# Plain fp32 products for the recurrent state of a state-space layer, and a second buffer for that state

## The chip, the core and the metric

The program runs on one core of a Trainium2 chip. A core has five engines that run side by side, each through its own list of instructions in a fixed order: TensorE (PE, matrix products, with PEld for the loading of its stationary operand), VectorE (DVE), ScalarE (ACT), GpSimd (POOL) and SyncE (SP, which here only issues transfers). An instruction waits until the semaphores that it names have been raised, and everything behind it on the same engine waits with it. The metric is the time of one execution on the device in microseconds (us), here the median of three runs. A profile is one execution taken by the hardware profiler.

## The reference, cut to what matters

Two layers are computed for 128 prompt tokens and 512 sample tokens. Layer 0 is attention, layer 1 a bidirectional state-space layer. The change touches only the chunked scan of layer 1:

```python
def ssd_chunked(x, a, b, c, h0):          # T tokens in chunks of 128, 4 groups of 8 heads
    a_cs = jnp.cumsum(a, axis=2)
    ...
    decay_end = jnp.exp(a_cs[:, :, -1:] - a_cs)
    states = jnp.einsum('bclgn,bclgrp->bcgrpn', b, x * decay_end[..., None])
    chunk_decay = jnp.exp(a_cs[:, :, -1])
    def step(h, inp):
        s, d = inp
        return h * d[..., None, None] + s, h
    h_final, h_prev = lax.scan(step, h0, (states, chunk_decay))
    y_off = jnp.einsum('bclgn,bcgrpn->bclgrp', c, h_prev) * jnp.exp(a_cs)[..., None]
    return y_diag + y_off, h_final
```

It is run forwards and backwards in time, with the same `b` and `c`. For each group of 8 heads the state `h` is a matrix of 128 (the state's width) by 512 (8 heads of 64). Each chunk reads it (`y_off`) and then replaces it by its decayed self plus that chunk's `states`.

## The kernel before

All large products have fp32 inputs that are split into a high and a low part (`split`, lines 72 to 74: the high part is a cast to the type fp32r on ACT, the low part is the input minus the high part, on DVE unless another engine is named). A product is then three products of parts, high by high, high by low and low by high, summed in PSUM. So it is for the projections (`proj_T`, line 914) and for the output product (`out_mm`, line 1400), and so it is, through `mm3` (lines 1010 to 1014), for the two products on the state. Products of smaller operands take fp32 as it is ("plain" below): the 128x128 product of B and C in `decay` (line 1131), the within-chunk product in `diag` (line 1149) and the prompt's final state (`prompt_state`, line 1175).

Layer 1 goes through 4 groups `g`. For a group, ten projections make x, B, C and z (`conv_chunk`, lines 994 to 999: three DVE steps, a tanh on ACT, one more DVE step). Then the scan runs over steps `j`, with `d` the direction:

- `weighted` (line 1163) makes x times its weights on POOL, and splits it into `xwh` and `xwl`;
- `off` (lines 1201 to 1208) multiplies C (`C0`, `C1` are its parts) by the state's parts `hh` and `hl`; DVE scales the result (line 1207), POOL adds it to `ys` (line 1208);
- `advance` (lines 1210 to 1217) multiplies B turned (`T0`, `T1`) by `xwh` and `xwl`; DVE multiplies the state by its decay in place (line 1215), adds the product (line 1216), and `h_split` splits the new state into `hh` and `hl` again.

`off` runs for four steps and two directions in each of 4 groups, 32 times; `advance` for three steps, 24 times. While the scan of group `g` runs, the projections of group `g + 1` are computed between its products (`fl`), so that TensorE has work while the scan waits. In the last group the output product takes their place.

The program is written in one order; a scheduler then sets the order of each engine's instructions by a cost model of its own, and puts in the waits. Tiles come from pools by tag: `hh`, `hl`, `xwh` and `xwl` have one buffer for each direction, `xw` one for both, and the state `h` one for each direction for the whole layer. PSUM tiles of the pool `pa` (tag `a`, 4 buffers) hold the products of the scan and all transposes; those of `pj` (2 buffers) the projections. At the layer's end the freed tiles hold parts of the output product's operand (`hold`) and of the gate (`mod_gate`).

In the trace a tile is named by its tag without what follows a figure: `h` is the state, and in rows of line 914 the projection's input.

Of the kernel before, what the change touches and what calls it, by code (L numbers as in the profile page):

```python
# [9 lines left out]
F32R = mybir.dt.float32r  # L10
AF = mybir.ActivationFunctionType
ALU = mybir.AluOpType
# [4 lines left out]
P = 128  # L17
D = 1024
KD = D // P
NT = 5  # L20
# [7 lines left out]
TW = 644  # L28
# [25 lines left out]
class Hybrid:  # L54
# [955 lines left out]
    def mm3(self, out, a, b, start=True, stop=True):  # L1010
        nc = self.nc
        nc.tensor.matmul(out, a[0], b[0], start=start, stop=False)
        nc.tensor.matmul(out, a[0], b[1], start=False, stop=False)
        nc.tensor.matmul(out, a[1], b[0], start=False, stop=stop)

    def layer1(self, hT, wp, pj, pa, ctx):
# [10 lines left out]
        bcs, xts, zss, W, Xw, H, Hs, St = {}, {}, {}, {}, {}, {}, {}, {}  # L1027
# [13 lines left out]
        def bc_unit(g, which):  # L1041
            if which == 0:
                wcur["bc"] = self.load_w(wp, A["l1_w_in"], [(2 * DI + P * g, P), (2 * DI + P * (NG + g), P)])
                bcs[g] = {"C": [self.tl(sp, [P, TW - 3], F32R, tag=f"C{i}") for i in range(2)]}
                bcs[g]["T"] = [self.tl(sp, [P, 4, P], F32R, tag=f"T{i}") for i in range(2)] + [self.tl(sp, [P, P], tag="T2")]
            u = wcur["u"] = bcs[g][which] = self.conv_chunk(16 + 4 * which + g, wcur["bc"], P * which, hT, pj, self.tl(sp, [P, TW - 3], tag=f"B{which}"))
            if which:
                self.split(*bcs[g]["C"], u, nc.gpsimd)

        def b_turn(g):  # L1050
            hi, lo, prompt = bcs[g]["T"]

            def put(t, ps):
                if t.start:
                    self.split(hi, lo, ps)
                else:
                    nc.scalar.copy(prompt, ps[:, 0, :])
            self.turn(bcs[g][0], pa, put)
# [97 lines left out]
        def weighted(g, t, d):  # L1156
            if t:
                xl = self.tl(wk, [P, 512], F32R, tag=f"xwl{d}", bufs=1)
                xh = self.tl(wk, [P, 512], F32R, tag=f"xwh{d}", bufs=1)
                xw = self.tl(wk, [P, 512], tag="xw", bufs=1)  # L1160
            else:
                xw = self.tl(wk, [P, 512], tag=f"xwl{d}", bufs=1)
            nc.gpsimd.tensor_tensor(h3(xw), h3(xts[g][:, t, :]), bch(self.ws[:, t, sl(g, d)]), op=ALU.mult)
            if t:
                self.split(xh, xl, xw)
                Xw[g, t, d] = (xh, xl)
            else:
                Xw[g, t, d] = xw

        def prompt_state(g, d):  # L1170
            xw = Xw.pop((g, 0, d))
            T = bcs[g]["T"]
            ps = self.tl(pa, [P, 4, P], tag="a")
            for j in range(4):
                nc.tensor.matmul(ps[:, j, :], xw[:, P * j:P * j + P], T[2], start=True, stop=True)
            st = self.tl(wk, [P, 4, P], tag="ym")
            nc.scalar.copy(st, ps)
            dst = O["new_state_f" if d == 0 else "new_state_b"][0, 8 * g:8 * g + 8].rearrange("h p n -> (h p) n").rearrange("(j q) n -> q j n", q=P)
            nc.sync.dma_start(out=dst, in_=st)
# [6 lines left out]
        def state_init(g, d):  # L1186
            st = St.pop((g, d))
            ps = self.tl(pa, [P, 4, P], tag="a")
            for j in range(4):
                nc.tensor.transpose(ps[:, j, :], st[:, j, :], self.ident)  # L1190
            h = H[d] = self.tl(sp, [P, 512], tag=f"h{d}")
            nc.scalar.copy(h, ps.rearrange("p j q -> p (j q)"))
            h_split(d)

        def h_split(d):
            hh = self.tl(wk, [P, 512], F32R, tag=f"hh{d}", bufs=1)
            hl = self.tl(wk, [P, 512], F32R, tag=f"hl{d}", bufs=1)
            self.split(hh, hl, H[d])
            Hs[d] = (hh, hl)

        def off(g, t, d):
            C = bcs[g]["C"]
            y = Y[:, t].rearrange("p j q -> p (j q)")
            ps = self.tl(pa, [P, 512], tag="a")
            self.mm3(ps, [C[i][:, ts(t)] for i in range(2)], Hs[d])
# [4 lines left out]
        def advance(g, t, d):  # L1210
            T = bcs[g]["T"]
            p2 = self.tl(pa, [P, 512], tag="a")
            self.mm3(p2, [T[i][:, t - 1, :] for i in range(2)], Xw.pop((g, t, d)))
            h = H[d]
            nc.vector.tensor_tensor(h3(h), h3(h), bch(self.cd[:, t, sl(g, d)]), op=ALU.mult)
            nc.vector.tensor_tensor(h, p2, h, op=ALU.add)
            h_split(d)
# [97 lines left out]
        def hold(t, q, tags, pool):  # L1315
            self.yT[t, q] = [self.tl(pool, [P, 4, P], F32R, tag=i, bufs=1) for i in tags]
            self.y_turn(t, q, wk, "u")
# [13 lines left out]
        for n in range(4, 6):  # L1331
            self.mod_gate(1, n, self.grow[1, n], pa, "a", wk, "xwh0", "xwl0")
# [10 lines left out]
        for k0 in range(0, 12, 2):  # L1343
# [3 lines left out]
            if k0 == 0:  # L1347
                hold(1, 1, ("hh0", "hl0"), wk)
                hold(4, 1, ("hh1", "hl1"), wk)
                hold(0, 1, ("xwh1", "xwl1"), wk)  # L1350
            elif k0 == 4:
                hold(1, 2, ("B0", "B1"), sp)
                hold(4, 2, ("C0", "C1"), sp)
                hold(0, 2, ("T0", "T1"), sp)
# [142 lines left out]
```

## Time and profile before

| | |
|---|---|
| Median of 3 runs | 1020.06 us (1019.86 to 1020.76) |
| Span of the profiled execution | 1016.4 us |
| Median less that span (start and end of a run, outside the trace) | 3.7 us |
| Busy share of the span: PE, PEld, DVE, ACT, POOL | 92%, 83%, 72%, 54%, 50% |
| Mean granted TensorE clock | 0.978 |

The profiled execution's own whole time is not listed, only its span from the first to the last instruction; 3.7 us is what lies around it if that execution was a median one. Busy time of PE counts a product from its start to its modelled end, which overlaps the start of the next one; the rate of a stream of products is therefore read from start to start. Layer 1's four groups lie at about 480 to 900 us, and the output product then takes the rest.

### The profile page before, as it was taken

The numbers are of one execution on the slowest core, as the hardware profiler recorded it, in microseconds if no ns is written. First come the engines' busy times: TensorE is split into PE (matmuls) and PEld (weight loads), VectorE is DVE, ScalarE is ACT, GpSimd is POOL, SyncE is SP. The second block draws the span as 40 slices with busy tenths as digits, with TensorE's granted clock in tenths as the row PEclk, the third lists the DMA queues.
The fourth block names the chain that finished last, engine by engine and source line by source line (L and its number), as shares of the span: only waits on it lengthen the run. The fifth ranks groups of instructions, "written<-read, shape, count | busy, mean of one in ns | idle before, by whom it ended". The sixth has DMA issues, their size and how long they took to land. (4 is left out here: it accounts for less than half of the span.)

```text
span 1016.4 us, 17297 instructions
## 1 busy us (share of the span) xinstructions
PE 939.4 (92%) x6522; PEld 847.7 (83%) x6522; DVE 727.0 (72%) x1094; ACT 549.4 (54%) x1272; POOL 503.2 (50%) x451
## 2 busy tenths in 40 slices
PE   5998999999999899989998898898988999889998
PEld 3898878989997789978997797788987999667786
DVE  5478665766776766757688788977688767996663
ACT  5346766757766653323465575567445664654340
POOL 3355325225450433445177679869487867642000
PEclk9999999999999999999999899998999999899999
DMA  9933242211122322333342345235324532446752
GB/s 312 350 120 104 92 142 89 84 52 43 42 64 84 104 87 102 125 100 96 99 137 91 104 147 171 68 129 160 111 90 133 178 110 89 135 147 193 256 194 100
DMA packets 90354, 127.91 MB, mean 126 GB/s; under 512 B 6816, under 2 KB 65312, under 8 KB 90272
## 3 DMA queue, kind: packets, MB, share of 16 engines
q1 hardware_dynamic: 90272, 126.82, 39.0%
q8 instruction: 51, 0.84, 0.3%
q14 instruction: 31, 0.25, 0.1%
HBM read 115.10 MB, written 11.70 MB: 125 GB/s over the span
## 5 line engine op out<-in xcount | busy, mean ns | idle before, releaser
L914 PE MATMUL pj<-h,wh 128*128 128x322 f32 (+1 forms) x1248 | 293.5, 320 | 6.2 <-DVE B L999 4.2
L74 POOL TENSOR_TENSOR wl<-raw,wh 128x512 fp32r<-128x512 f32 (+1 forms) x70 | 135.6, 1949 | 183.5 <-ACT wh L73 183.3
L914 PEld LDWEIGHTS pj<-h,wh 128*128 128x128 f32 (+1 forms) x1248 | 214.9, 192 | 11.0 <-issue 4.4
L914 PE MATMUL pj<-h,wl 128*128 128x322 f32 (+1 forms) x624 | 198.0, 318 | 0.0
L73 ACT CAST wh<-raw 128x1024 fp32r<-128x1024 f32 (+1 forms) x117 | 103.3, 912 | 81.8 <-DMA raw<-in_l_w_out 26.0
L914 PEld LDWEIGHTS pj<-h,wl 128*128 128x128 f32 (+1 forms) x624 | 120.2, 193 | 1.2 <-issue 0.2
L1140 ACT ACTIVATE am<-am,nb 128x128 f32<-128x128 f32 x320 | 98.6, 392 | 28.4 <-POOL am L1135 14.2
L283 PE MATMUL pp<-wh,big 128*128 128x256 f32 x576 | 113.4, 287 | 0.5 <-ACT sg L527 0.5
L283 PEld LDWEIGHTS pp<-wh,big 128*128 128x128 f32 x576 | 92.4, 191 | 0.7 <-ACT sg L527 0.7
L74 DVE TENSOR_TENSOR wl<-raw,wh 128x1024 fp32r<-128x1024 f32 x47 | 68.9, 1470 | 26.7 <-ACT wh L73 26.6
L283 PE MATMUL pp<-wl,big 128*128 128x256 f32 x288 | 81.8, 284 | 0.0
L74 DVE TENSOR_TENSOR pl<-pt,ph 128x512 fp32r<-128x512 f32 (+1 forms) x100 | 59.2, 600 | 25.9 <-ACT ph L73 25.0
L633 DVE TENSOR_REDUCE nm<-S 128x1 f32<-128x640 f32 x64 | 52.4, 820 | 13.6 <-PE S L630 12.7
L73 ACT CAST ph<-pt 128x512 fp32r<-128x512 f32 (+1 forms) x100 | 51.3, 518 | 18.8 <-PE pt L658 14.1
L637 ACT ACTIVATE Pt<-S,nm 128x640 f32<-128x640 f32 x64 | 51.3, 803 | 12.1 <-PE pt L658 9.5
L1141 POOL TENSOR_TENSOR am<-am,am 128x1024 f32<-128x1024 f32 x20 | 50.2, 2512 | 14.6 <-ACT am L1140 14.0
L1208 POOL TENSOR_TENSOR ys<-ys,ym 128x512 f32<-128x512 f32 x32 | 48.8, 1533 | 13.6 <-DVE ym L1207 13.6
L283 PEld LDWEIGHTS pp<-wl,big 128*128 128x128 f32 x288 | 55.0, 191 | 0.0
L658 PE MATMUL pt<-cst,Pt 128*128 128x128 f32 x320 | 50.8, 276 | 2.7 <-DVE pl L74 2.3
L630 PE MATMUL S<-kT,qT 128*128 128x320 f32 x256 | 50.6, 322 | 1.4 <-ACT Pt L637 1.4
L841 PE MATMUL a<-wh,big 128*128 128x256 f32 x256 | 46.8, 283 | 0.0
L658 PEld LDWEIGHTS pt<-cst,Pt 128*128 128x128 f32 x320 | 36.6, 141 | 11.9 <-PE S L630 3.8
(375 smaller groups left out, 2319.8 us busy)
## 6 DMA issues: line engine op xcount, KB each, us to landing
raw<-in_l_w_in SPq DMA_DIRECT2D x48, 512.0 KB
am<-acd SPq DMA_DIRECT2D x40, 512.0 KB
raw<-in_l_w_out SPq DMA_DIRECT2D x36, 512.0 KB
og<-in_l_mod_w SPq DMA_DIRECT2D x29, 512.0 KB
raw<-in_l_w_in SPq DMA_DIRECT2D x25, 256.0 KB
mw<-in_l_mod_w SPq DMA_DIRECT2D x11, 512.0 KB
raw<-in_l_mod_w SPq DMA_DIRECT2D x8, 512.0 KB
yzd<-ys SPq DMA_DIRECT2D x6, 640.0 KB
```

Of the source, the lines that this page charges most:

```text
L73: (heng.tensor_copy if heng else self.nc.scalar.copy)(hi, src)
L74: (eng or self.nc.vector).tensor_tensor(lo, src, r32(hi), op=ALU.subtract)
L283: nc.tensor.matmul(ps, a[:, k, cs], b[:, k, :], start=k == 0 and a is hi and b is w[0], stop=k == KD - 1 and a is lo)
L630: nc.tensor.matmul(S[:, 192 + 320 * q:512 + 320 * q], qTs[g, t][:, h, :], kT[:, hl, 320 * q:320 * q + 320], start=hl == 0, stop=hl == 1)
L633: nc.vector.tensor_reduce(c["m"], c["s"], axis=AX.X, op=ALU.max, negate=True)
L637: nc.scalar.activation(Pt, c["s"], AF.Exp, bias=c["m"], scale=1.0, accum_out=rss[g][t][:, h:h + 1])
L658: nc.tensor.transpose(pt[:, 2 * i + j, :], Pts[j][:, kt * P:kt * P + P], self.ident)
L841: self.nc.tensor.matmul(ps, self.ohl[a][:, k, ts], w[b][:, k, :], start=k == 0 and i == 0, stop=k == KD - 1 and i == 2)
L914: nc.tensor.matmul(ps[0:m, 190 + 322 * half:512 + 322 * half], w[b][:, k, off:off + m], hT[s][:, k, 322 * half:322 * half + 322], start=fi ...
L1140: nc.scalar.activation(af[d][:, h, :], af[d][:, h, :], AF.Exp, bias=self.nb[:, t, i:i + 1], scale=1.0)
L1141: nc.gpsimd.tensor_tensor(af[0], af[0], af[1], op=ALU.add)
L1208: nc.gpsimd.tensor_tensor(y, y, m, op=ALU.add)
```

## The change

The two products on the state become one plain fp32 product each. With `mm3` go all splits of the state, of the weighted x, of C, and of the turned B; the fp32 tiles of C (`bcs[g][1]`) and of the turned B (`T`, one tile for all five chunks now) are the operands. The state is no longer updated in place: each step takes a new buffer of two (`bufs=2`), the decay's product goes from the old into the new one, and the sum is made in the new one. The weighted x gets two buffers for each direction. The tags of `hold` and `mod_gate` follow. In the changed kernel's own numbering the product of `off` is line 1172 and its scaling 1174, the product of `advance` is line 1179, the decay 1182 and the sum 1183; `conv_chunk` keeps its lines.

```diff
-    def mm3(self, out, a, b, start=True, stop=True):
-        nc = self.nc
-        nc.tensor.matmul(out, a[0], b[0], start=start, stop=False)
-        nc.tensor.matmul(out, a[0], b[1], start=False, stop=False)
-        nc.tensor.matmul(out, a[1], b[0], start=False, stop=stop)
...
-            if which:
-                self.split(*bcs[g]["C"], u, nc.gpsimd)
...
-            hi, lo, prompt = bcs[g]["T"]
-
-            def put(t, ps):
-                if t.start:
-                    self.split(hi, lo, ps)
-                else:
-                    nc.scalar.copy(prompt, ps[:, 0, :])
-            self.turn(bcs[g][0], pa, put)
+            T = bcs[g]["T"]
+            self.turn(bcs[g][0], pa, lambda t, ps: nc.scalar.copy(T[:, t, :], ps))
...
+            xw = Xw[g, t, d] = self.tl(wk, [P, 512], tag=f"xw{d}", bufs=2)
             nc.gpsimd.tensor_tensor(h3(xw), h3(xts[g][:, t, :]), bch(self.ws[:, t, sl(g, d)]), op=ALU.mult)
-            if t:
-                self.split(xh, xl, xw)
-                Xw[g, t, d] = (xh, xl)
-            else:
-                Xw[g, t, d] = xw
...
-            h = H[d] = self.tl(sp, [P, 512], tag=f"h{d}")
-            nc.scalar.copy(h, ps.rearrange("p j q -> p (j q)"))
-            h_split(d)
-
-        def h_split(d):
-            hh = self.tl(wk, [P, 512], F32R, tag=f"hh{d}", bufs=1)
-            hl = self.tl(wk, [P, 512], F32R, tag=f"hl{d}", bufs=1)
-            self.split(hh, hl, H[d])
-            Hs[d] = (hh, hl)
+            H[d] = self.tl(wk, [P, 512], tag=f"h{d}", bufs=2)
+            nc.scalar.copy(H[d], ps.rearrange("p j q -> p (j q)"))
 
         def off(g, t, d):
-            C = bcs[g]["C"]
             y = Y[:, t].rearrange("p j q -> p (j q)")
             ps = self.tl(pa, [P, 512], tag="a")
-            self.mm3(ps, [C[i][:, ts(t)] for i in range(2)], Hs[d])
+            nc.tensor.matmul(ps, bcs[g][1][:, ts(t)], H[d], start=True, stop=True)
...
         def advance(g, t, d):
-            T = bcs[g]["T"]
             p2 = self.tl(pa, [P, 512], tag="a")
-            self.mm3(p2, [T[i][:, t - 1, :] for i in range(2)], Xw.pop((g, t, d)))
-            h = H[d]
-            nc.vector.tensor_tensor(h3(h), h3(h), bch(self.cd[:, t, sl(g, d)]), op=ALU.mult)
+            nc.tensor.matmul(p2, bcs[g]["T"][:, t, :], Xw.pop((g, t, d)), start=True, stop=True)
+            old, h = H[d], self.tl(wk, [P, 512], tag=f"h{d}", bufs=2)
+            H[d] = h
+            nc.vector.tensor_tensor(h3(h), h3(old), bch(self.cd[:, t, sl(g, d)]), op=ALU.mult)
             nc.vector.tensor_tensor(h, p2, h, op=ALU.add)
-            h_split(d)
```

The scheduler's order moves with it. On TensorE, at the second scan step of group 0, before: the parts of the state (`hh0`, `hl0` forwards, `hh1`, `hl1` backwards) by C, the weighted x by the turned B, and projections of group 1 (line 914).

```order
L1012 MATMUL a_1455_7037<-hh0_1434_6899,C0_1387_6598 128x512
L1013 MATMUL a_1455_7037<-hl0_1435_6900,C0_1387_6598 128x512
L1014 MATMUL a_1455_7037<-hh0_1434_6899,C1_1388_6599 128x512
L1012 MATMUL a_1457_7044<-hh1_1437_6909,C0_1387_6598 128x512
L1013 MATMUL a_1457_7044<-hl1_1438_6910,C0_1387_6598 128x512
L1014 MATMUL a_1457_7044<-hh1_1437_6909,C1_1388_6599 128x512
L1012 MATMUL a_1459_7051<-xwh0_1446_6962,T0_1389_6600 128x512
L1013 MATMUL a_1459_7051<-xwl0_1445_6961,T0_1389_6600 128x512
L1014 MATMUL a_1459_7051<-xwh0_1446_6962,T1_1390_6601 128x512
```

The same place on TensorE after the change, where B1 is C in fp32, T the turned B and xw0, xw1 the weighted x:

```order
L1172 MATMUL a_1437_6992<-h0_1422_6868,B1_1392_6663 128x512
L914 MATMUL pj_1456_7059<-h10_1183_5264,wh_1452_7049 128x322
L1172 MATMUL a_1439_6997<-h1_1424_6873,B1_1392_6663 128x512
L1179 MATMUL a_1441_7002<-xw0_1431_6924,T_1387_6598 128x512
L1179 MATMUL a_1443_7007<-xw1_1432_6926,T_1387_6598 128x512
```

Three instructions have become one in each product, and no instruction that waits for a low part stands between a state's product and the next. On DVE, at the same step before, from the last operation of a projection's chunk to the scaling of the decay matrix `am0`:

```order
L999 SCALAR_TENSOR_TENSOR u_1451_6973<-pj_1452_6974,u_1451_6973 128x641
L74 TENSOR_TENSOR hl0_1435_6900<-h0_1405_6747,hh0_1434_6899 128x512
L74 TENSOR_TENSOR hl1_1438_6910<-h1_1409_6758,hh1_1437_6909 128x512
L1215 TENSOR_TENSOR h0_1405_6747<-h0_1405_6747,cd_1346_6373 128x512
L74 TENSOR_TENSOR xwl1_1448_6967<-xw_1450_6969,xwh1_1449_6968 128x512
L1154 TENSOR_TENSOR ys_1310_6019<-ys_1310_6019,a_1442_6950 128x512
L1215 TENSOR_TENSOR h1_1409_6758<-h1_1409_6758,cd_1346_6373 128x512
L1142 TENSOR_TENSOR am0_1414_6797<-am0_1414_6797,cb_1440_6915 128x1024
```

And after the change on DVE, from the same operation of that chunk to the next chunk's first:

```order
L999 SCALAR_TENSOR_TENSOR u_1433_6928<-pj_1434_6929,u_1433_6928 128x641
L1174 TENSOR_TENSOR ym_1438_6994<-a_1437_6992,ea_1345_6372 128x512
L1174 TENSOR_TENSOR ym_1440_6999<-a_1439_6997,ea_1345_6372 128x512
L1183 TENSOR_TENSOR h0_1442_7004<-a_1441_7002,h0_1442_7004 128x512
L1182 TENSOR_TENSOR h0_1464_7134<-h0_1442_7004,cd_1346_6373 128x512
L1183 TENSOR_TENSOR h1_1444_7009<-a_1443_7007,h1_1444_7009 128x512
L1182 TENSOR_TENSOR h1_1466_7139<-h1_1444_7009,cd_1346_6373 128x512
L994 TENSOR_SCALAR u_1455_7058<-pj_1456_7059,cw_99_556,cols_21_110 128x641
```

The three low parts are gone from the step, and the decay of the next state (into its other buffer, `h0_1464` from `h0_1442`) follows the sum at once.

## Rows read from the trace of the kernel before

**Rows 1.** Page, busy time of an engine, its share of the span, instructions.
```profile
PE 939.4 (92%) x6522; PEld 847.7 (83%) x6522; DVE 727.0 (72%) x1094; ACT 549.4 (54%) x1272; POOL 503.2 (50%) x451
```

**Rows 2.** Busy time by stretch of layer 1: us, each engine, granted clock, DMA.
```profile
core 0: us, PE busy (x) PEld busy (x) DVE busy (x) ACT busy (x) POOL busy (x), PEclk, DMA share, GB/s
480.00:900.00 420.00, 387.62 (x2562) 358.08 (x2561) 336.71 (x366) 239.48 (x565) 300.29 (x193) 0.97 0.39 122
540.00:560.00 20.00, 15.83 (x81) 13.27 (x79) 19.46 (x20) 7.56 (x24) 14.40 (x10) 0.91 0.24 84
...
620.00:640.00 20.00, 16.09 (x102) 13.31 (x101) 19.02 (x18) 8.51 (x19) 20.00 (x14) 1.00 0.42 138
640.00:660.00 20.00, 16.22 (x86) 14.19 (x86) 20.00 (x21) 10.01 (x27) 15.59 (x10) 0.91 0.29 80
...
860.00:880.00 20.00, 15.19 (x89) 12.23 (x90) 20.00 (x22) 10.86 (x24) 15.24 (x10) 0.91 0.27 89
```

**Rows 3.** Waits of PE, 480 to 900 us: us in total, times, longest.
```profile
PE a L1013 <- DVE hl L74: 8.2, 7, 2.9
PE a L1012 <- DVE ys L1154: 4.7, 2, 2.7
PE pj L914 <- DVE B L999: 4.2, 3, 2.8
...
PE a L1013 <- DVE xwl L74: 2.4, 1, 2.4
PE a L1012 <- ACT hh L73: 2.3, 2, 1.3
...
PE a L1012 <- DVE h L1216: 0.8, 1, 0.8
```

**Rows 4.** Timeline of DVE from 538 us: start, us, operation, idle before.
```profile
539.30 4.66 DVE L74 TENSOR_TENSOR hl<-h,hh 128x512 fp32r<-128x512 f32 x2
543.89 2.87 DVE L1215 TENSOR_TENSOR h<-h,cd 128x512 f32<-128x512 f32 x1
```

**Rows 5.** Groups on DVE, 480 to 930 us: count, busy us, mean ns, idle before.
```profile
L74 DVE TENSOR_TENSOR hl<-h,hh 128x512 fp32r<-128x512 f32 x32 | 41.6, 1315 | 3.6 <-ACT hh L73 3.3
...
L1215 DVE TENSOR_TENSOR h<-h,cd 128x512 f32<-128x512 f32 x24 | 28.0, 1174 | 0.0
L74 DVE TENSOR_TENSOR xwl<-xw,xwh 128x512 fp32r<-128x512 f32 x24 | 27.9, 1161 | 3.3 <-ACT xwh L73 3.3
...
L1216 DVE TENSOR_TENSOR h<-a,h 128x512 f32<-128x512 f32 x24 | 16.3, 677 | 0.0
```

**Rows 6.** Timeline of PE: one product in three parts, and the next start.
```profile
530.04 0.40 PE L1012 MATMUL a<-xwh,T 128*128 128x512 f32 x1
530.28 0.39 PE L1013 MATMUL a<-xwl,T 128*128 128x512 f32 x1
530.51 0.40 PE L1014 MATMUL a<-xwh,T 128*128 128x512 f32 x1
530.75 0.39 PE L1012 MATMUL a<-xwh,T 128*128 128x512 f32 x1
```

**Rows 7.** Timeline of PE: plain products (two records each), and the next start.
```profile
486.55 0.43 PE L962 MATMUL a<-am,xs 128*128 128x160 f32 x2
486.82 0.43 PE L963 MATMUL a<-am,xs 128*128 128x160 f32 x2
...
585.14 1.05 PE L1175 MATMUL a<-T,xwl 128*128 128x128 f32 x8
586.03 0.39 PE L1131 MATMUL a<-B,B 128*128 128x128 f32 x2
```

**Rows 8.** Waits of DVE and of POOL, 480 to 930 us: us in total, times, longest.
```profile
DVE am L1142 <- POOL am L1141: 9.8, 6, 5.2
...
POOL xw L1163 <- DVE xwl L74: 11.4, 8, 2.6
```

More of the change, by code (lines that the diff above doesn't have):

```diff
@@ L1026, in layer1 @@
         Y = self.Y = self.tl(sp, [P, NT, 4, P], tag="ys")
-        bcs, xts, zss, W, Xw, H, Hs, St = {}, {}, {}, {}, {}, {}, {}, {}
+        bcs, xts, zss, W, Xw, H, St = {}, {}, {}, {}, {}, {}, {}
         wcur = {}
@@ L1043, in bc_unit @@
                 wcur["bc"] = self.load_w(wp, A["l1_w_in"], [(2 * DI + P * g, P), (2 * DI + P * (NG + g), P)])
-                bcs[g] = {"C": [self.tl(sp, [P, TW - 3], F32R, tag=f"C{i}") for i in range(2)]}
-                bcs[g]["T"] = [self.tl(sp, [P, 4, P], F32R, tag=f"T{i}") for i in range(2)] + [self.tl(sp, [P, P], tag="T2")]
-            u = wcur["u"] = bcs[g][which] = self.conv_chunk(16 + 4 * which + g, wcur["bc"], P * which, hT, pj, self.tl(sp, [P, TW - 3], tag=f"B{which}"))
-            if which:
-                self.split(*bcs[g]["C"], u, nc.gpsimd)
-        def b_turn(g):
-            hi, lo, prompt = bcs[g]["T"]
-            def put(t, ps):
-                if t.start:
-                    self.split(hi, lo, ps)
-                else:
-                    nc.scalar.copy(prompt, ps[:, 0, :])
-            self.turn(bcs[g][0], pa, put)
+                bcs[g] = {"T": self.tl(sp, [P, NT, P], tag="T")}
+            wcur["u"] = bcs[g][which] = self.conv_chunk(16 + 4 * which + g, wcur["bc"], P * which, hT, pj, self.tl(sp, [P, TW - 3], tag=f"B{which}"))
+        def b_turn(g):
+            T = bcs[g]["T"]
+            self.turn(bcs[g][0], pa, lambda t, ps: nc.scalar.copy(T[:, t, :], ps))
         def z_tile(g, jj):
@@ L1156, in weighted @@
         def weighted(g, t, d):
-            if t:
-                xl = self.tl(wk, [P, 512], F32R, tag=f"xwl{d}", bufs=1)
-                xh = self.tl(wk, [P, 512], F32R, tag=f"xwh{d}", bufs=1)
-                xw = self.tl(wk, [P, 512], tag="xw", bufs=1)
-            else:
-                xw = self.tl(wk, [P, 512], tag=f"xwl{d}", bufs=1)
-            nc.gpsimd.tensor_tensor(h3(xw), h3(xts[g][:, t, :]), bch(self.ws[:, t, sl(g, d)]), op=ALU.mult)
-            if t:
-                self.split(xh, xl, xw)
-                Xw[g, t, d] = (xh, xl)
-            else:
-                Xw[g, t, d] = xw
+            xw = Xw[g, t, d] = self.tl(wk, [P, 512], tag=f"xw{d}", bufs=2)
+            nc.gpsimd.tensor_tensor(h3(xw), h3(xts[g][:, t, :]), bch(self.ws[:, t, sl(g, d)]), op=ALU.mult)
         def prompt_state(g, d):
@@ L1174, in prompt_state @@
             for j in range(4):
-                nc.tensor.matmul(ps[:, j, :], xw[:, P * j:P * j + P], T[2], start=True, stop=True)
+                nc.tensor.matmul(ps[:, j, :], xw[:, P * j:P * j + P], T[:, 0, :], start=True, stop=True)
             st = self.tl(wk, [P, 4, P], tag="ym")
@@ L1315, in hold @@
         def hold(t, q, tags, pool):
-            self.yT[t, q] = [self.tl(pool, [P, 4, P], F32R, tag=i, bufs=1) for i in tags]
+            self.yT[t, q] = [self.tl(pool, [P, 4, P], F32R, tag=i, bufs=1 if tags[0] != tags[1] else 2) for i in tags]
             self.y_turn(t, q, wk, "u")
@@ L1331, in layer1 @@
         for n in range(4, 6):
-            self.mod_gate(1, n, self.grow[1, n], pa, "a", wk, "xwh0", "xwl0")
+            self.mod_gate(1, n, self.grow[1, n], pa, "a", wk, "xw0", "xw0", 2)
         part_mm(12)
@@ L1347, in layer1 @@
             if k0 == 0:
-                hold(1, 1, ("hh0", "hl0"), wk)
-                hold(4, 1, ("hh1", "hl1"), wk)
-                hold(0, 1, ("xwh1", "xwl1"), wk)
+                hold(1, 1, ("h0", "h0"), wk)
+                hold(4, 1, ("h1", "h1"), wk)
+                hold(0, 1, ("xw1", "xw1"), wk)
             elif k0 == 4:
@@ L1353, in layer1 @@
                 hold(4, 2, ("C0", "C1"), sp)
-                hold(0, 2, ("T0", "T1"), sp)
+                hold(0, 2, ("T", "T1"), sp)
             elif k0 == 8:
```

## Prediction

> **What bounds the kernel now.** I read the page's first part: TensorE (PE) is busy for 92% of the span and DVE for 72% [rows 1]. Such a share is a mean over stages, so I went on to the stretches of layer 1 [rows 2]. From 480 to 900 us, where the four scans lie, PE is busy for 387.6 of 420 us, and its idle 32.4 us are not spread evenly: from 540 to 560, 640 to 660 and 860 to 880 us PE falls to 15.8, 16.2 and 15.2 of 20 while DVE stands at 19.5, 20.0 and 20.0. There DVE is the bound. In the same three stretches the granted clock is 0.91: after each gap PE runs for a while at 1.2 instead of 2.4 GHz. Over the 420 us the clock is 0.97, and the 3% that lack are worth 0.03 x 420 = 12.6 us of full speed. So 32.4 + 12.6 = 45 us of PE's time is the most that can come back here.
>
> Next the waits name who held PE up [rows 3]. Waits on the parts of the operands that the change removes: 8.2 us for `hl`, 2.4 for `xwl`, 2.3 for `hh`, and 0.8 for the state itself, together 13.7. Waits on DVE work that has nothing to do with the split but stood in the same queue: 4.7 us for the sum into `ys` (line 1154, it frees a PSUM tile) and 4.2 for a chunk's last step (line 999), together 8.9. The timeline shows how the queue comes about [rows 4]: from 539.30 us two `hl` subtractions take 4.66 us, and the decay in place behind them 2.87 us. By the groups [rows 5] the sum with one operand in PSUM (line 1216) has a mean of 677 ns, while `hl`, `xwl` and the decay of the same size, whose operands all lie in SBUF, have 1315, 1161 and 1174 ns. They are lengthened by something, and they run while POOL is busy too [rows 2].
>
> **The change part by part.** *PE.* The split product on 512 columns costs 530.75 - 530.04 = 0.71 us from start to start in an unbroken stream [rows 6]. Plain products of 512 columns are not in this trace; narrower ones are [rows 7]: 160 columns go from 486.55 to 486.82, 0.27 us, which makes 0.86 us for 512, and four products of 128 columns take 586.03 - 585.14 = 0.89 us for 512 in all. From below, a plain product leaves two records, and if each passed at the split part's rate (0.71 / 3 = 0.24 us) it would cost 0.47 us. I take 0.87, between the two that were seen. There are 32 + 24 = 56 products, so PE gains work: 56 x (0.87 - 0.71) = +9.0 us (ends: -13.4 and +10.1). That is the surprise in this change: one instruction instead of three, and slower.
>
> The Trainium skill ("FP8 and Floating Point Precision", section TensorE Precision Notes) states that true fp32 makes four passes through the array. Four passes at 0.24 us are 0.95 us by an estimate from that page and the stream above, +13.3 us in all, and the sum below would end at 1009.2 us. The 0.27 us for 160 columns agree with four passes of 160 columns at 2.4 GHz, without the overhead of a split part's start.
>
> *DVE.* The 32 subtractions for `hl` and 24 for `xwl` go: 41.6 + 27.9 = 69.5 us of 336.7 in the stretch [rows 2, 5], 21% of DVE's load, and they lie just in the steps in which it is full. Without them the three full stretches would not be full. The state's path gets shorter by a cast and a subtraction: product, sum, next product.
>
> Of the 13.7 us of waits on parts I let 3 us return as waits on the sum alone: -10.7 us. Of the 8.9 us in DVE's queue I let three quarters go, because DVE's load falls by a fifth where it was at 97 to 100%: -6.7 us. With 17.4 of 32.4 us of idle time gone I take the same share of what the clock costs: 17.4 / 32.4 x 12.6 = -6.8 us. The other 10 us of idle time (waits on POOL's and ACT's results) I leave as they are.
>
> The Trainium skill ("SBUF — State Buffer", section Who interferes with whom) says that a DVE instruction with two SBUF inputs contends with a GpSimd instruction that reads SBUF, and that the loser is blocked until the other is through. That fits 1315 against 677 ns. By it the lengthening is a wait that the next such instruction inherits, so DVE would be relieved only by 56 x 0.677 = 38 us instead of 69.5; scaling the 6.7 us by that gives 3.7, the clock's share falls to 5.6, and the sum would end at 1009.
>
> *What I cost at nothing.* 60 casts on ACT (`hh`, `xwh`, the high part of C) and four subtractions on POOL go; ACT is busy for 239 of 420 us, so its work is hidden beside PE's, and this matters only through the waits counted above. The turned B is copied instead of cast, on the same engine. The second buffer of the state removes no wait of before: the decay in place never left DVE idle (0.0 in its group, [rows 5]). It prevents a new one: `off` now reads the state itself on PE, and a decay in place would have to wait for that product, with DVE's chunk steps queued behind it. With two buffers the decay waits for a product that was issued a step earlier. The two buffers of the weighted x free POOL from its 11.4 us of waiting for `xwl` [rows 8]; POOL's results then come a little earlier, which I don't count. The one wait on PE that takes the place of the old ones is that of `off` for the sum. Behind it stand the projections of the next group, whose results DVE, ACT and then the next weights' PSUM tiles wait for. In the new order of group 0 some 22 projection products (0.15 us each, by 322 of 512 columns of 0.24) stand between one step's products and the next `off`, over 3 us, against two sums and the decay between them, 0.68 us each, that DVE has to do meanwhile (the two scalings run beside the products of `advance`); DVE meets that when nothing else stands before them, so the 3 us that I let return are not zero. The end (`hold`, `mod_gate`) gets its tiles from tags whose last readers are scan products done before; if a reader were late, only the output product's operand would wait, a few us at most.
>
> *The sum.* +9.0 - 10.7 - 6.7 - 6.8 = -15.2 us. From the span 1016.4 - 15.2 = 1001.2, with 3.7 us around it 1004.9 us. The profiled execution is taken as a median one, since its span and those 3.7 us are set to make 1020.06.
>
> **The rivals.** *POOL sets the step.* With DVE freed, the scan waits for POOL, which multiplies x by its weights, masks and adds the decays and adds into `ys`. For it: POOL is busy for 20.0 of 20 us from 620 to 640 [rows 2], and DVE itself waited 9.8 us for its decay sums [rows 8]. Against it: over the stretch POOL has 300 of 420 us, and where PE was lowest (860 to 880) it has 15. Then the queue's waits stay and only those on parts go, with their share of the clock: -10.7 - 10.7 / 32.4 x 12.6 + 9.0 = -5.9, 1014.2 us.
>
> *PE pays and gets nothing back: slower.* TensorE is the bound at 92%, and each plain product holds it 0.16 us longer. If the new order lets `off` wait for the sum for as long as it waited for the parts (in the new order the four products of a step stand together, and the sum of the second direction comes last in DVE's queue), the whole +9.0 us stays: 1029.1 us. It decides for slower from the point at which less than 7 of the 45 us come back. Against it: 13.7 us are put down by name to what is removed.
>
> *Nothing to be seen.* 7 to 11 us come back and pay for the passes: 1018 to 1022 us.
>
> *All comes back.* PE is never idle and always at full clock: 9.0 - 45 = -36, 984 us. The same time comes out of the forecast if a plain product costs its lower end (-24.2 - 13.4 = -37.6, 982.5 us). Against the first: 10 us of idle time have other causes; against the second: both rows of plain products.
>
> **How the numbers follow.** Forecast (995 to 1012) 0.52; POOL's step (1012 to 1018) 0.16; all back or a cheap product (below 995) 0.11; nothing to be seen 0.08; slower 0.13. What a measurement of this kernel can tell from no change is about 0.2%, 2 us. So faster 0.52 + 0.16 + 0.11 = 0.79, same 0.08, slower 0.13. The range from 990 to 1022 leaves out the lower part of "all back" and most of "slower", some 0.18.
>
> **What would show it.** Right: in the new trace a plain product of 512 columns takes 0.85 to 0.9 us from start to start; DVE's busy time from 480 to 900 us falls by 40 to 70 us; no stretch of 20 us has DVE above 19; PE's idle time there is 15 us or less and the clock 0.98 or more; waits of PE on the sum of the state add up to about 3 us. Wrong: PE's idle time is as large as before and put down to the state's sum or to POOL; or the plain product costs 0.5 or 1 us, which moves the time by 56 times the difference.

## The result, and the profile after

The changed kernel takes 1005.42 us (median of 4 runs, 1004.66 to 1006.87) against 1019.96 us for the kernel before, run on the same chip (4 runs, 1015.28 to 1020.76). The ratio is 0.9874 with a 95% interval of 0.9852 to 0.9897: faster by 14.5 us, where 1004.9 us had been forecast. A later repeat of both gave 0.9883 (0.9851 to 0.9916). The span of the profiled execution fell from 1016.4 to 1003.1 us.

The page's line of busy times, after:

```profile
PE 935.6 (93%) x6466; PEld 832.5 (83%) x6466; DVE 667.6 (67%) x1034; ACT 515.1 (51%) x1212; POOL 500.0 (50%) x447
```

Against [rows 1], DVE lost 60 instructions and 59 us (the 56 subtractions and, not counted in the prediction, four for the low part of the turned B, 2.7 us together); PE has 56 records fewer (two for a product instead of three) and nearly the same busy time. The price of a plain product stands in the timeline of PE, after (start, duration, records):

```profile
523.05 1.88 PE L1172 MATMUL a<-h,B 128*128 128x512 f32 x4
524.77 1.02 PE L1179 MATMUL a<-xw,T 128*128 128x512 f32 x2
```

Four records are two products, and the next starts 1.72 us later: 0.86 us each, against 0.71 for three parts [rows 6].

The same stretches as in [rows 2], after:

```profile
480.00:900.00 420.00, 394.26 (x2562) 351.41 (x2561) 293.45 (x325) 213.14 (x518) 299.73 (x196) 0.98 0.41 127
540.00:560.00 20.00, 18.15 (x84) 14.03 (x83) 18.99 (x20) 8.50 (x25) 17.77 (x12) 0.91 0.35 105
620.00:640.00 20.00, 15.96 (x95) 13.26 (x95) 17.89 (x23) 9.03 (x22) 18.76 (x15) 0.91 0.39 117
860.00:880.00 20.00, 17.54 (x86) 13.33 (x86) 19.93 (x21) 10.65 (x22) 10.56 (x6) 0.91 0.52 171
```

DVE falls by 43 us, but one stretch is still full (19.93), and PE is still idle for 25.7 us. A fixed stretch compares unlike work, though: after, some 13 us of the output product's work have moved into it. The next two fences hold the same work, from the turning of B in group 0 to the last product of the output's first part; of before, and of after:

```profile
512.80:942.70 429.90, 393.62 (x2531) 356.55 (x2529) 351.27 (x385) 247.17 (x571) 299.85 (x204) 0.97 0.40 128
```

```profile
514.20:929.00 414.80, 389.84 (x2475) 342.00 (x2474) 292.74 (x325) 213.25 (x511) 296.18 (x200) 0.98 0.42 132
```

The instruction counts fit the change (2531 - 2475 = 56; 385 - 325 = 60). The work takes 15.1 us less: PE's idle time fell from 36.3 to 25.0 us, 11.3, and its busy time by 3.8, although the plain products add 56 x 0.15 = 8.4. DVE fell by 58.5 us.

Waits of PE from 480 to 900 us, after (us, times, longest):

```profile
PE a L1371 <- POOL ssq L1098: 4.3, 1, 4.3
PE a L1116 <- DVE h L1183: 4.0, 1, 4.0
PE pj L914 <- DVE B L999: 3.8, 3, 2.4
PE a L1137 <- DVE h L1183: 2.4, 1, 2.4
PE pj L914 <- DVE u L999: 1.8, 1, 1.8
```

Of [rows 3] the waits on parts are gone, and so is that on `ys`; the one on L999 is not. Two new ones name the sum L1183, 6.4 us together, but the waiting instructions are not products with the state: L1116 (B by C) and L1137 (the turning of `ys`) write into PSUM tiles of the same four buffers, and read nothing that the sum makes: what they lack is the tile that it empties.

Groups on DVE, 480 to 930 us, as in [rows 5], after; behind them three of before that were not shown:

```profile
L1127 DVE TENSOR_TENSOR am<-am,cb 128x1024 f32<-128x1024 f32 x20 | 40.0, 2001 | 6.7 <-POOL am L1126 6.2
L1182 DVE TENSOR_TENSOR h<-h,cd 128x512 f32<-128x512 f32 x24 | 28.8, 1211 | 0.1
L1086 DVE TENSOR_TENSOR ys<-ys,zs 128x512 f32<-128x512 f32 x12 | 18.3, 1534 | 0.3
L1183 DVE TENSOR_TENSOR h<-a,h 128x512 f32<-128x512 f32 x24 | 15.8, 679 | 1.5 <-PE a L1179 1.5
L1086 DVE TENSOR_TENSOR ys<-ys,zs 128x128 f32<-128x128 f32 x12 | 12.9, 1082 | 0.0
```

```profile
L1142 DVE TENSOR_TENSOR am<-am,cb 128x1024 f32<-128x1024 f32 x20 | 34.8, 1740 | 10.1 <-POOL am L1141 9.8
L1101 DVE TENSOR_TENSOR ys<-ys,zs 128x512 f32<-128x512 f32 x12 | 13.6, 1149 | 0.2
L1101 DVE TENSOR_TENSOR ys<-ys,zs 128x128 f32<-128x128 f32 x12 | 10.0, 842 | 0.1
```

Of the other operations with two SBUF inputs these got longer: the mask's product by 5.2 us in all, the gate by 4.7 and 2.9, the decay by 0.8, together 13.6. But one got shorter, the low part of the weights; over the same work, before and after:

```profile
L74 DVE TENSOR_TENSOR wl<-raw,wh 128x1024 fp32r<-128x1024 f32 x28 | 45.9, 1638 | 15.4 <-ACT wh L73 15.4
```

```profile
L74 DVE TENSOR_TENSOR wl<-raw,wh 128x1024 fp32r<-128x1024 f32 x28 | 38.7, 1382 | 12.0 <-ACT wh L73 12.0
```

With it and the smaller ones, the operations that are left took some 7 us more on balance. That is half of what lacks between the 72.2 us taken away (69.5 and 2.7) and the 58.5 that DVE was relieved of. For the other half an estimate is the overlap of neighbours, which busy time counts once: operations of 0.68 us start 0.60 us apart where they follow each other (619.48 to 620.08 in a timeline below), and 60 of them are gone. The sum with an operand in PSUM stayed at 679 ns.

What lengthens an operation can be read from these traces. In those of before, of the changed kernel and of the run with the subtractions put back (below), from 480 to 930 us, DVE has 184 operations of 128x512 with two SBUF inputs (low parts, decays, subtractions put back). Of the 55 beside which POOL was idle throughout, all took 0.67 to 0.69 us; all 104 that took over 0.75 us ran beside a busy POOL. Of the 168 with an input in PSUM (scalings and sums), all took 0.67 to 0.69 us, though POOL was busy for over half of the time of 124. So it is the two SBUF inputs beside a busy POOL.

### The profile page after: what moved, and what is told of

The parts are those of the page before. It is cut to its first block, busy times and chain, and to the rows that moved or that the text cites. A ratio compares the mean times of both kernels' runs of the same rounds, so it can differ in the third digit from the quotient of the medians.

```text
span 1003.1 us, 17041 instructions
## 1 busy us (share of the span) xinstructions
PE 935.6 (93%) x6466; PEld 832.5 (83%) x6466; DVE 667.6 (67%) x1034; ACT 515.1 (51%) x1212; POOL 500.0 (50%) x447
## 4 chain that ended last, share of the span: by engine, by line
PE 54%; DVE 14%; POOL 11%; issue 8%; DMA 7%; ACT 6%; SPq 0%; POOLq 0%; DVEq 0%; ACTq 0%
PE pj L914 14%; PE pp L283 8%; PE po L668 3%; PE a L841 3%; PE pj L1366 3%; PE acc L379 3%; PE S L630 3%; PE pt L658 3%; DMA am<-acd 2%; PE pp L175 2%; POOL ys L1175 2%; POOL am L1126 2%; POOL xw L1143 2%; DVE ys L1086 2%; ACT am L1125 2%
## 5 line engine op out<-in xcount | busy, mean ns | idle before, releaser
L914 PE MATMUL pj<-h,wh 128*128 128x322 f32 (+1 forms) x1248 | 299.4, 326 | 7.3 <-DVE B L999 3.8
L914 PEld LDWEIGHTS pj<-h,wh 128*128 128x128 f32 (+1 forms) x1248 | 212.3, 190 | 19.4 <-issue 12.6
L74 POOL TENSOR_TENSOR wl<-raw,wh 128x512 fp32r<-128x512 f32 (+1 forms) x70 | 131.8, 1893 | 185.1 <-ACT wh L73 183.4
L74 DVE TENSOR_TENSOR wl<-raw,wh 128x1024 fp32r<-128x1024 f32 x47 | 61.6, 1317 | 23.7 <-ACT wh L73 23.6
L1366 PE MATMUL pj<-wh,h 128*128 128x512 f32 x160 | 52.5, 402 | 1.0 <-ACT h L73 1.0
```

What stands on the lines that cost most here:

```text
L74: (eng or self.nc.vector).tensor_tensor(lo, src, r32(hi), op=ALU.subtract)
L914: nc.tensor.matmul(ps[0:m, 190 + 322 * half:512 + 322 * half], w[b][:, k, off:off + m], hT[s][:, k, 322 * half:322 * half + 322], start=fi ...
L1366: nc.tensor.matmul(self.PS[t][n], y[a][:, kk, :], b, start=k0 + k == 0 and i == 0, stop=k0 + k == 15 and i == 2)
```

## The experiments

Each ran beside the kernel before on its chip; since chips differ a little, the ratios to it are what is compared, and the kernel before has medians from 1015.98 to 1019.96 us on them.

**What a plain product costs TensorE.** First each plain product was issued twice, onto the same result:

```
-            nc.tensor.matmul(ps, bcs[g][1][:, ts(t)], H[d], start=True, stop=True)
+            for _ in range(2):
+                nc.tensor.matmul(ps, bcs[g][1][:, ts(t)], H[d], start=True, stop=True)
...
-            nc.tensor.matmul(p2, bcs[g]["T"][:, t, :], Xw.pop((g, t, d)), start=True, stop=True)
+            xw = Xw.pop((g, t, d))
+            for _ in range(2):
+                nc.tensor.matmul(p2, bcs[g]["T"][:, t, :], xw, start=True, stop=True)
```

> The changed kernel with each of the 56 plain products on the state issued twice into the same place of PSUM: 56 x 0.86 = 48 us more of TensorE's work, nothing more elsewhere. Theory (TensorE is the bound for most of the scan once VectorE is relieved): 30 to 48 us slower than the changed kernel, 1035 to 1053 us. Rival (another engine sets the scan's pace and TensorE's idle 26 us there take the work up): at most 25 us slower, 1030 us or less.

Measured: 1035.48 us, ratio 1.0176 (1.0143 to 1.0209), 30 us over the changed kernel. The timeline of PE in this kernel:

```profile
521.19 3.60 PE L1173 MATMUL a<-h,B 128*128 128x512 f32 x8
524.63 1.88 PE L1182 MATMUL a<-xw,T 128*128 128x512 f32 x4
```

Eight records, four products, 3.44 us: 0.86 again. The 56 more products are 48 us of PE's work, and 30 of them show. Over the same work PE's idle time is 13.0 us in this kernel, against 25.0:

```profile
512.40:958.60 446.20, 433.25 (x2586) 361.95 (x2585) 286.84 (x327) 214.21 (x511) 291.31 (x200) 0.99 0.39 123
```

So 12 of the other 18 us went into idle time; a part of the rest is the clock, 0.99 for 0.98.

Then the opposite, one pass in place of a plain product:

```
-                bcs[g] = {"T": self.tl(sp, [P, NT, P], tag="T")}
+                bcs[g] = {"T": self.tl(sp, [P, NT, P], F32R, tag="T")}
...
-            xw = Xw[g, t, d] = self.tl(wk, [P, 512], tag=f"xw{d}", bufs=2)
+            xw = Xw[g, t, d] = self.tl(wk, [P, 512], F32R, tag=f"xw{d}", bufs=2)
...
-            old, h = H[d], self.tl(wk, [P, 512], tag=f"h{d}", bufs=2)
+            old, h = H[d], self.tl(wk, [P, 512], F32R, tag=f"h{d}", bufs=2)
```

> The changed kernel with the four operands of the products on the state rounded to fp32r where they are made, and one product in one part: it leaves out the low parts, and with them part of the precision. TensorE loses 56 x (0.86 - 0.24) = 35 us of work, nothing else changes. Theory (the passes are paid in full): 20 to 35 us faster than the changed kernel, 970 to 985 us. Rival (VectorE and POOL set the pace in the scan, the passes are hidden beside them): 10 us or less, 995 us and up.

Measured: 976.57 us, ratio 0.961 (0.9577 to 0.9643). The timeline of PE:

```profile
521.33 0.63 PE L1172 MATMUL a<-h,B 128*128 128x512 f32 x2
521.79 0.39 PE L1179 MATMUL a<-xw,T 128*128 128x512 f32 x1
```

Two products in 0.46 us, 0.23 each: 56 x (0.86 - 0.23) = 35 us less work, and 29 us less time (27 by the ratios). Work on TensorE shows for the greater part, 29 of 35 here and 30 of 48 there, and the step of the sum that charged the passes holds. The forecast had worked with four passes of 0.24 us as one of its cases (the Trainium skill, "FP8 and Floating Point Precision", section TensorE Precision Notes). By an estimate from that page, reckoned as the forecast did on 160 columns, four passes of 512 columns at 2.4 GHz take 4 x 512 / 2.4 = 853 ns, and the measured 0.86 us agrees. Too dear in that case of the forecast were the 0.24 us for a pass.

**Is it VectorE's load that came back as time?** The 56 subtractions were put back on DVE, with two SBUF inputs and results that nothing reads:

```
+        def back(d, src):
+            dm = self.tl(wk, [P, 512], tag=f"dm{d}", bufs=1)
+            nc.vector.tensor_tensor(dm, src, src, op=ALU.subtract)
...
             nc.vector.tensor_tensor(h, p2, h, op=ALU.add)
+            back(d, h)
```

(the same behind the first state and, but for the prompt, behind the weighted x).

> The changed kernel with 56 subtractions of 128 by 512 put back on VectorE, each with two SBUF inputs and on the places where the low parts were made; nothing reads their results, so no product waits for one. Theory (VectorE's queue): the 6.7 us in that queue and their share of the clock return, some 9 us: 1010 to 1017 us. Rival (only the waits on parts mattered, VectorE's load did not): 0 to 2 us, 1005 to 1007 us.

Measured: 1016.53 us (10 runs), ratio 0.9975 (0.9952 to 0.9998). Nearly the whole gain is gone, though no product waits for these results. The same work as above takes 428.4 us, PE idle 33.0, DVE 348:

```profile
513.30:941.70 428.40, 395.42 (x2475) 343.64 (x2474) 347.95 (x380) 212.99 (x511) 296.70 (x200) 0.98 0.41 128
```

The theory was DVE's time in the queue, 58 us of it. A second form was to tell load from contention: 56 subtractions of the same size, behind each scaling and each sum, but with one input in PSUM:

```
             nc.vector.tensor_tensor(h3(m), h3(ps), bch(self.ea[:, t, sl(g, d)]), op=ALU.mult)
+            back(d, ps, m)
...
             nc.vector.tensor_tensor(h, p2, h, op=ALU.add)
+            back(d, p2, h)
```

> As the run that puts 56 subtractions back on VectorE, but each has one operand in PSUM (the product's result), so it is expected to take about 0.68 us whatever POOL does: 38 us of VectorE's work. Theory (it is VectorE's whole queue time that counts, lengthened by POOL): half of what the run with two SBUF inputs gives back, 3 to 6 us, 1008 to 1011 us. Rival (the lengthening is inherited by the next instruction, so both kinds of subtraction load VectorE alike): as slow as that run, 1010 to 1017 us.

Measured: 1000.55 us, ratio 0.9831 (0.9796 to 0.9867). Neither theory: in this kernel 37 us of added DVE work cost nothing. The groups on DVE, 480 to 930 us, of the first form and of the second:

```profile
L1143 DVE TENSOR_TENSOR dm<-h 128x512 f32<-128x512 f32 x32 | 34.3, 1071 | 1.4 <-ACT h L1173 1.3
L1143 DVE TENSOR_TENSOR dm<-xw 128x512 f32<-128x512 f32 x24 | 24.2, 1026 | 0.0
```

```profile
L1143 DVE TENSOR_TENSOR dm<-a,ym 128x512 f32<-128x512 f32 x32 | 21.4, 682 | 0.3
L1143 DVE TENSOR_TENSOR dm<-a,h 128x512 f32<-128x512 f32 x24 | 16.0, 678 | 0.1
```

With a PSUM input each takes 0.68 us, with two SBUF inputs a half more, because some of these run beside a busy POOL (the counts above). This agrees with the rule that the prediction cited (the Trainium skill, "SBUF — State Buffer", section Who interferes with whom); no run here took POOL's work away. By the busy time alone the first form would cost 58 and the second 37 us of DVE, and a queue that hurts at 58 should hurt somewhat at 37; it did not. That points to the kind of operation, but does not show it: the places differ too. In the first form all 56 stand between a step's first sum (or the group's first state) and the scalings of the next step; in the second 32 stand behind the scalings and only 24 behind the sums. The second form ran in one order alone. No run put operations of either kind in the places of the other.

Since an added instruction also moves the order of all others, the first form was repeated in another order, that of the fastest version with two buffers (below), against its 998.98 us:

> The changed kernel with its decays behind the scalings (999.0 us), and with the 56 subtractions of two SBUF inputs whose results nothing reads put on VectorE. If their price is that of their kind (VectorE beside GpSimd, some 60 us of busy time): 1008 to 1014 us, about the 11 us that they cost in the changed kernel's own order. If the 11 us there were an accident of that order, as the 56 subtractions from PSUM hint, which cost nothing: 996 to 1002.

Measured: 1015.69 us (10 runs), ratio 0.9966 (0.9946 to 0.9986): 17 us more than that order without them (16 by the ratios). The waits of PE, 480 to 900 us, in this kernel:

```profile
PE a L1116 <- DVE ym L1183: 9.7, 4, 5.4
PE a L1007 <- DVE u L999: 5.0, 3, 2.3
PE a L1137 <- DVE h L1193: 4.7, 5, 2.2
```

Here L1183 is the scaling and L1193 the sum: in the first and the third row PE lacks PSUM tiles that DVE empties late; in the second it waits for a chunk's last step in DVE's queue. In two orders, then, these 56 operations cost 11 and 17 us, and taking them away is where the kernel's gain is from. Whether by their kind or by their places stays open.

**Half of the change.** `off` plain and `advance` in three parts, and the reverse; each with the casts and subtractions that its split half needs, and two buffers of the state in both. The edit of the first, where the products are issued:

```
-            self.mm3(ps, [C[i][:, ts(t)] for i in range(2)], Hs[d])
+            nc.tensor.matmul(ps, bcs[g][1][:, ts(t)], H[d], start=True, stop=True)
```

> Only the product that reads the state (off) is plain; the product that updates it keeps its three parts, so the 32 subtractions for the state's low part go and the 24 for the weighted x stay. Theory (VectorE's load and the waits on parts share the return of some 24 us): 32 products pay 0.15 us each, 4.8 us; 41.6 of 69.5 us of VectorE's load go, 60% of 24 us is 14.5; 1020 - 14.5 + 4.8 = 1010 us. Rival (only the waits on parts count, 11.3 of 13.7 us of them on the state's parts): 1020 - 20 + 4.8 = 1005 us, as fast as the changed kernel.

> Only the product that updates the state (advance) is plain; the one that reads it keeps its three parts, so the state and C are still split, the weighted x and the turned B are not. Theory: 24 products pay 0.15 us, 3.6 us; 27.9 of 69.5 us of VectorE's load go, 40% of 24 us is 9.7; 1020 - 9.7 + 3.6 = 1014 us. Rival (only waits on parts count, 2.4 of 13.7 us of them on the weighted x): 1020 - 4 + 3.6 = 1019 us, no change from the kernel before.

Measured: 1002.24 us, ratio 0.9826 (0.9791 to 0.9862), and 1007.11 us, ratio 0.9871 (0.983 to 0.9912). Three of the four expectations were too slow; the rival for the first half, 1005 of 1020 us or 0.985, lies inside the interval. Either half alone returns about what the whole does (0.9874). The parts don't add up: the whole may hold something that costs what the second half should bring, or the orders of the three kernels differ by as much. The next runs ask this of the state's buffer.

**The second buffer of the state.** The changed kernel with the state updated in place:

```
-            old, h = H[d], self.tl(wk, [P, 512], tag=f"h{d}", bufs=2)
-            H[d] = h
-            nc.vector.tensor_tensor(h3(h), h3(old), bch(self.cd[:, t, sl(g, d)]), op=ALU.mult)
+            h = H[d]
+            nc.vector.tensor_tensor(h3(h), h3(h), bch(self.cd[:, t, sl(g, d)]), op=ALU.mult)
```

> The changed kernel with the state updated in place again, one buffer as before: the decay on VectorE has to wait for the plain product that reads the state. Theory (a full VectorE queue was the bound, and the second buffer only prevents a new wait): 1 to 5 us slower than the changed kernel, 1006 to 1010 us, with a wait of VectorE's decay on the product that was not there. Rival (the second buffer is itself a good part of the gain): 6 us or more slower, 1011 us and up.

(The tag keeps its two buffers, which the groups now take in turn; within a group the state stays in one.)

Measured: 996.07 us, ratio 0.9769 (0.973 to 0.9808). Both theories fell, mine most: in place the kernel is 9 us faster (11 by the ratios), and its decays never left DVE idle: the wait that was expected is not there. The timeline of DVE in the changed kernel, at the start of group 1 (start, duration):

```profile
613.25 2.15 DVE L1182 TENSOR_TENSOR h<-h,cd 128x512 f32<-128x512 f32 x1
615.33 3.93 DVE L1086 TENSOR_TENSOR ys<-ys,zs 128x512 f32<-128x512 f32 x2
619.18 1.77 DVE L1182 TENSOR_TENSOR h<-h,cd 128x512 f32<-128x512 f32 x1
620.88 0.94 DVE L994 TENSOR_SCALAR u<-pj,cw,cols 128x641 f32<-128x641 f32 x1
...
623.57 0.68 DVE L1183 TENSOR_TENSOR h<-a,h 128x512 f32<-128x512 f32 x1
624.29 0.81 DVE L1182 TENSOR_TENSOR h<-h,cd 128x512 f32<-128x512 f32 x1
625.02 0.68 DVE L1174 TENSOR_TENSOR ym<-a,ea 128x512 f32<-128x512 f32 x1
```

and PE beside it:

```profile
614.69 1.02 PE L1172 MATMUL a<-h,B 128*128 128x512 f32 x2
615.55 1.88 PE L1179 MATMUL a<-xw,T 128*128 128x512 f32 x4
...
624.31 0.79 PE L1116 MATMUL a<-B,B 128*128 128x128 f32 x2 [4.04 <-DVE h L1183]
```

The four products of this step were done by 617.4 us, but until 623.57 DVE emptied none of their tiles: two decays and the gate, all of them long, and three chunk steps stand ahead. With a second buffer a decay is ready as soon as the state before it is, and the order on DVE takes it early: the group's third decay, which is the next step's (624.29), even stands ahead of its first scaling (625.02).

To tell the buffer from the order, both buffers stay and each decay is queued behind the scaling of its step and direction (the program's order follows from this anew):

```
-            nc.vector.tensor_tensor(h3(m), h3(ps), bch(self.ea[:, t, sl(g, d)]), op=ALU.mult)
+            Sc[d] = nc.vector.tensor_tensor(h3(m), h3(ps), bch(self.ea[:, t, sl(g, d)]), op=ALU.mult)
...
-            nc.vector.tensor_tensor(h3(h), h3(old), bch(self.cd[:, t, sl(g, d)]), op=ALU.mult)
+            with tc.issue_after(Sc[d].ins):
+                nc.vector.tensor_tensor(h3(h), h3(old), bch(self.cd[:, t, sl(g, d)]), op=ALU.mult)
```

> The changed kernel with both buffers of the state, and only the order on VectorE altered: each decay is queued behind the scaling of the same step and direction, so that it stands about where it stands with the state updated in place. Theory (the second buffer costs by the place it gives the decays: they are ready early, stand ahead of the scalings that empty PSUM tiles, and TensorE then lacks a tile): 994 to 999 us, as in place (996.1), and the decays' place in group 1 gives most of it. Rival (the second buffer costs by itself, by the memory it takes or the addresses it moves, or the 9 us between the two kernels are another part of the order): 1003 to 1007.

Its reference on the same chip is the changed kernel once more:

> The changed kernel as it is, beside the runs above on the same chip: 1003 to 1007 us, against which the other three are read.

Measured: 998.98 us, ratio 0.9808 (0.9785 to 0.9832), against 1006.93 us, 0.9883 (0.9851 to 0.9916). With both buffers in place another order gives back 8 us, so the buffer by itself is not the cause, and the order is. The same work as above in this kernel, and DVE at the start of group 1 (scaling L1176, decay L1185, sum L1186):

```profile
513.60:922.10 408.50, 389.66 (x2475) 342.15 (x2474) 295.85 (x326) 214.88 (x511) 292.12 (x200) 0.98 0.43 135
```

```profile
611.15 5.11 DVE L1086 TENSOR_TENSOR ys<-ys,zs 128x512 f32<-128x512 f32 x2
...
618.88 0.68 DVE L1176 TENSOR_TENSOR ym<-a,ea 128x512 f32<-128x512 f32 x1
619.48 0.68 DVE L1185 TENSOR_TENSOR h<-h,cd 128x512 f32<-128x512 f32 x1
620.08 0.68 DVE L1176 TENSOR_TENSOR ym<-a,ea 128x512 f32<-128x512 f32 x1
```

Against 414.80 us it is 6.3 us less, PE's busy time is the same within 0.2 us, and its idle time falls from 25.0 to 18.8: all of the difference is waiting that is gone. Between gate and first emptied tile there are now three chunk steps and no decay. The gate itself comes earlier too, which no single edit of mine did: it follows from the new order as a whole. How much of the 8 us is the decays' place is therefore not shown. In the kernels of two runs above, the subtractions with a PSUM input (1000.55 us) and the first half (1002.24 us), every decay stands ahead of its step's scalings as it does in the changed kernel, and they are no slower than it (0.9831 and 0.9826 for 0.9874).

How far back should the decay go? Behind the scalings of both directions (`Sc[1]` in place of `Sc[d]`):

> As the run before, but each decay is queued behind the scalings of both directions of its step. Theory (scalings first is what counts): 993 to 999 us, no worse than behind one. Rival (the decay then reaches the sum too late, and the sum holds the advance product's PSUM tile): 1000 to 1006, since the two decays of 1.2 us each stand between scaling and sum in every step.

Measured: 1007.73 us, ratio 0.9907 (0.9871 to 0.9943): as slow as the changed kernel, and a little beyond the rival's range. The waits of PE, 480 to 900 us, of this kernel, and of the one before it:

```profile
PE a L1137 <- DVE h L1186: 8.5, 4, 3.4
```

```profile
PE a L1137 <- DVE h L1186: 3.8, 4, 1.6
```

Now the sum L1186 comes late and holds the tile of `advance`, as the rival said; that is 4.7 of the 8.7 us between the two kernels. Last, the decay of the kernel before behind its scaling, in the same way:

> The kernel before (three products, high and low parts, state updated in place) with each decay queued behind the scaling of its step and direction. If the place of the decay costs the kernel before as much as the changed one, it comes to 1007 to 1012 us against 1016 to 1020, and half of what the change gained could have been had without it. Rival (in the kernel before the parts of the state are what TensorE waits for, and a later decay makes the sum and the parts later): 1018 to 1026.

Measured: 1028.91 us, ratio 1.0107 (1.0082 to 1.0131), slower by 10.7 us. The rival was right: what helps the plain kernel harms the split one. The waits of PE, 480 to 900 us, in this run, and two of its stretches:

```profile
PE a L1149 <- DVE h L1219: 4.4, 1, 4.4
PE a L1012 <- ACT hh L73: 4.3, 3, 1.9
```

```profile
580.00:600.00 20.00, 12.95 (x73) 11.03 (x72) 14.43 (x15) 14.27 (x40) 13.88 (x8) 0.74 0.45 145
620.00:640.00 20.00, 14.71 (x69) 12.39 (x69) 15.62 (x14) 11.51 (x27) 18.78 (x13) 0.74 0.35 113
```

The sum comes later, the cast `hh` behind it too (4.3 us of waiting, 2.3 before [rows 3]), and PE's gaps lower its granted clock to 0.74 in two stretches. So the gain is no mere matter of order that the kernel before could have had by the same edit.

## Why the prediction was right, and where it was not

*The passes.* Right: 0.86 us for 0.87, +8.4 us for +9.0. The doubling and the one-pass run bear it out from both sides.

*The waits on parts, -10.7 us.* The 13.7 us went. In their place 3 us were to return as waits of `off` on the sum; none did there, but 6.4 us came as waits for PSUM tiles that the sum empties. The term is mis-sized by 3 us, and its reason was wrong: a product's result has to be taken out of PSUM, and that stands in the same queue. Nor is it a price by itself. With the subtractions put back no product waits for a part, and the gain was gone nearly whole (0.9975): this term and the next are one, the time of DVE's queue.

*The queue, -6.7 us.* The 4.7 us on `ys` went, the 4.2 us on the chunk's last step did not (3.8 and 1.8 after). So of the 17.4 us of idle time 11.3 came back over the same work. "DVE's load falls by a fifth" is at best half of the cause. A load of 58 us put back in the old form cost nearly all of the gain, one of 37 in another form and in other places cost nothing.

*The clock, -6.8 us.* The mean granted clock rose from 0.978 to 0.984: by 0.022 x 1016.4 - 0.016 x 1003.1 that is 6.3 us. These are one execution each: over the four of the changed kernel the clock is 0.980 to 0.984, which is 4 us, so the agreement is no closer than that.

*The sum.* By these measured terms it would be 8.4 - 11.3 - 6.3 = -9.2 us, and the span fell by 13.3, the same work by 15.1. The rest, 4 to 6 us, lies inside what counts as PE's busy time, where a product's end is modelled. A good part of it can be estimated: over the same work PE stands idle in 39 gaps before and in 16 after, and ahead of each a last part counts as busy for 0.40 us where the stream goes on after 0.24 [rows 6], so 23 gaps fewer make 23 x 0.16 = 3.7 us. Up to 2 us stay open. That 1004.9 us came so near is in part luck: too much idle time was counted as gone, and this rest was not counted at all.

*The second buffer.* Wrong. It was to prevent a wait of the decay for `off`; in place no such wait showed (996.07 us). With the buffer the kernel got an order, decays ahead of what empties PSUM among other things, that costs 8 to 9 us. I had read the order for where products stand and not for where the decays went. This is part of why the mark of PE's idle time (25.7 us, for 15) was missed: over the same work it is 18.8 for 25.0 with the decay behind its scaling. It is not why a full DVE stretch is left (19.93): in that run too DVE is busy for 19.96 of 20 us from 540 to 560 us, and PE for 18.07.

*The rivals.* POOL's step and the slower case are out by the time, and the cheap product by its 0.86 us. The case by which the lengthening is inherited ended at 1009; the mechanism is seen in part (some 7 us on balance went over to other operations), but DVE was relieved of 58.5 us, not of 38. Why either half alone returns as much as the whole was not settled; that orders of one work differ by 9 us and more makes such differences possible without another cause.

The versions that beat both kernels are the changed one with its state in place, 0.9769, and with two buffers and the decay behind its scaling, 0.9808; their intervals overlap.

## What to carry to other kernels

Ask of a vector operation where its inputs lie, who works beside it and what it stands ahead of, not for its busy time alone: those with two SBUF inputs beside a busy POOL, ahead of what empties PSUM, were worth taking away here. A second buffer takes a wait away and so lets an instruction go early; look in the engine's order at what it now stands ahead of, above all at what empties PSUM. And where a plain fp32 product replaces three parts, charge it to TensorE: the gain is only what the casts and subtractions held up.

## What was unexpected of the hardware

- One plain fp32 product on 512 columns takes 0.86 us, three single passes 0.71, one pass 0.23: the plain one is dearer than the three.
- 56 operations of 128x512 on DVE cost 11 and 17 us with two SBUF inputs (1.03 to 1.07 us each in the first of these runs), and nothing with one in PSUM (0.68 us each), in other places of the queue.
- An operation of 128x512 on DVE with two SBUF inputs took 0.67 to 0.69 us whenever POOL was idle beside it (55 of 55), and up to 2.97 us where it was not; one with an input in PSUM took 0.67 to 0.69 us always (168 of 168).
- A full DVE need not lower TensorE's clock: from 540 to 560 us in the run with PSUM inputs DVE is busy for 19.89 of 20 us, PE for 17.96 at a granted clock of 1.00 (before, the stretch at 640 us: 20.00, 16.22 and 0.91 [rows 2]):

```profile
540.00:560.00 20.00, 17.96 (x86) 12.71 (x85) 19.89 (x21) 7.86 (x23) 15.48 (x11) 1.00 0.33 106
```
